# A decoder trunk on one core: the hand-over from the up product to the down product of the ConvFFN is reordered

## The chip, the cores and the metric

The kernel runs on one NeuronCore of a Trainium2 chip. Its engines are PE (TensorE, matrix products), DVE (VectorE), ACT (ScalarE), POOL (GpSimd) and SP (SyncE, which here only issues DMAs). Each engine works through its own instructions in a fixed order and waits, instruction by instruction, on semaphores; ACT and POOL can issue DMAs too. The metric is the device time of one execution in microseconds (us).

## The reference

One inference step of a decoder trunk in float32: 1,024 prompt tokens behind 16 meta tokens, and 8 × 4 sample tokens, through a convolution layer, a shared latent-attention layer, and a ConvFFN in each of the two layers. What matters here is the ConvFFN, which both layers run:

```python
def conv_ffn(x, prefix, w_up, w_dw, w_down):
    h, tail = causal_dwconv(x @ w_up, prefix, w_dw)      # x: tokens x 1024, w_up: 1024 x 5632, 3 taps
    g, u = jnp.split(h, 2, axis=-1)                      # 2816 each
    return (jax.nn.silu(g) * u) @ w_down, tail           # w_down: 2816 x 1024

for layer in range(2):
    ...
    d_p, t_p = conv_ffn(rms_norm(hp, norm_ffn[layer]), zero_ffn, *f_params)
    d_s, t_s = conv_ffn(rms_norm(hs, norm_ffn[layer]), state_ffn_conv[layer], *f_params)
    hp, hs = hp + d_p, hs + d_s
```

The rows `tail` (the last up-projected rows) are outputs as well, `o["tail_f"]` in the kernel.

## The kernel before

Every float32 product is made of three: an operand is split into a rounded high part and the remainder (`split`: ACT writes the high part at L134, DVE the low part at L135), and PE adds high·high, high·low and low·high. So every operand of a product costs one ACT and one DVE instruction before PE can use it. Tokens lie along the free axis, 1,074 of them in layer 0 (1,062 in layer 1), features along the 128 partitions.

**The up product (`rise`).** 22 blocks f of 128 gate features and 128 up features. Each block is a product of 2 × 2 quarters done with seven products (L735) in place of eight; the operands are `b11`, `b21`, `b22`, `t1` to `t4` (made once, in the pool `xc`), and `product` runs them in the order t1, t2, b21, t3, then the next block's b11, then t4, b22. `keep` copies a partial sum out of PSUM on ACT (L743: `u2`, `u3`, `p1`), `join` adds it on DVE into the two rows `ub` of the block (L746). A product that goes on in the same PSUM bank waits for that copy: t3 for the copy of `u2`.

`tail(f)` then does, for the two rows: a store of the tail to `o["tail_f"]` (L700, SP's queue), the first tap on ACT (`c`, L703), two more taps on DVE (L705), the sample tokens on POOL, silu on ACT (L717), the product of the two on DVE (L718), and the store of the result to DRAM (`d_a[f]`, L719, SP's queue). The tiles `c` come from a pool of two buffers, which the RMS of the attention's cache (`nk`, eight odd blocks f of layer 0) borrows too, and gives back when its store `d_ss<-nk` has landed.

**The down product (`fall`).** It begins when `rise` is over, and its tiles are taken in the pools that `open_x` opens anew. `act(f)` loads `d_a[f]` back (L851, `raw`, three buffers) and splits it into `xh`/`xl`; `weight` loads a block of w_down (L151) and splits it into `wh`/`wl`. The 22 blocks f are the contraction now, in three groups (`BLOCKS`): 8, 7 and 7. In a group, for each of the eight output tiles, `gemm` (L170) runs over the blocks k of the group, three chunks of the tokens for each of the three products, so nine matmuls per k; DVE adds the result to `x` (L866), which is loaded back from `d_r` (L860).

```python
        for f in range(BLOCKS[0][1]):
            act(f)
        ...
            for ot in range(KD):
                w = self.weight(a["wdn"][layer, ot][:, f0 * 128:(f0 + n) * 128], n * 128)
                _, ps = self.gemm(w, [acts[f][0] for f in range(f0, f0 + n)], ...)
```

"The switch" below is the stretch between the last b22 product of `rise` and PE at full pace in `fall`. The order of each engine's instructions is set by a scheduler when the program is built, from the order of the code, priorities (`high_priority`) and ordering edges (`follow`, which cost no semaphore); where a tile lies, and so which earlier work it must wait for, follows from the order in which pools are opened and tiles taken.

Of the kernel before, what the change touches and what calls it, by code (L numbers as in the profile page):

```python
# [9 lines left out]
F32 = mybir.dt.float32  # L10
# [107 lines left out]
class Prog:  # L118
# [40 lines left out]

    def gemms(self, ws, mh, ml, off, tn, every=0):  # L160
        nc = self.nc
        ch = tn // 3
        cnt = 0
        ps = [self.pp.tile([128, 3, 512], F32, name="ps") for _ in ws]
        n = len(mh)
        for k in range(n):
            for w, p in zip(ws, ps):
                for i, (s, m) in enumerate(((w[0], mh), (w[0], ml), (w[1], mh))):
                    for c in range(3):
                        nc.tensor.matmul(p[:, c, :ch], s[:, k * 128:(k + 1) * 128], m[k][:, off + c * ch:off + (c + 1) * ch],  # L170
                                         start=k == 0 and i == 0, stop=k == n - 1 and i == 2)
                        cnt += 1
                        if every and cnt % every == 0:
                            next(self.fill, None)
        return [(p, p[:, :, :ch]) for p in ps]
# [114 lines left out]

    def open_x(self, tw=T0):
        self.tw = tw
        self.es_r, self.es_x, self.es_w, self.es_p = [self.top.enter_context(ExitStack()) for _ in range(4)]
        self.rp = self.pool(self.es_r, "rp", 1)
        self.xa, self.xb = [self.pool(self.es_x, n, 1) for n in ("xa", "xb")]
        self.xp = self.pool(self.es_w, "xp", 1)
        self.wp = self.pool(self.es_w, "wp", 2)
        self.tp = self.pool(self.es_w, "tp", 3)
        self.sp = self.pool(self.es_w, "sp", 1)

# [10 lines left out]
    def xhl(self, k):  # L311
        return self.xp.tile([128, self.tw], F32R, name=f"xh{k}"), self.xp.tile([128, self.tw], F32R, name=f"xl{k}")

# [198 lines left out]
    def layer_norm(self, ys):  # L512
# [15 lines left out]
        with self.tc.high_priority(PRIO):  # L528
            for k in range(KD):
                nc.vector.scalar_tensor_tensor(out=v3(ys[k]), in0=mu[:, :, :ch], scalar=-1.0 / D, in1=v3(ys[k]), op0=ALU.mult, op1=ALU.add)  # L530
            for k in range(KD):
                if k == 0:
                    self.sq_add(sq, ys[k], 0, T0)
                    continue
                q = self.xp.tile([128, self.tw], F32R, name=f"xl{k}").bitcast(F32)
                nc.scalar.activation(q, ys[k], AF.Square)
# [74 lines left out]
    def ffn(self, layer, xs, rstd, tn, done, extra=None):  # L611
        with ExitStack() as es:
            self.rise(es, layer, xs, rstd, tn, extra)
        self.es_r.close()
        self.open_x(self.tw)
        self.open_pp(self.es_p)
        with ExitStack() as es:
            self.fall(es, layer, tn, done)

    def rise(self, es, layer, xs, rstd, tn, extra):  # L620
# [20 lines left out]
        def operand(name, k, src, tag=None):  # L641
            h, l = [xc.tile([128, 536], F32R, name=f"{name}{x}{k}", tag=f"{tag or name}{x}{k}")[:, :hw] for x in "hl"]
            B[name, k] = h, l
            return self.split(h, l, src)[1]
# [49 lines left out]
        def tail(f):  # L694
# [3 lines left out]
            for j, ub in enumerate(ubs):  # L698
                t = f + j * NF
                nc.sync.dma_start(o["tail_f"][layer, t], ub[:, pe - 2:])  # L700
                nc.gpsimd.tensor_copy(sb[:, j, 16:48], ub[:, pe:])  # L701
                c = self.tp.tile([128, T0], F32, name="c", tag="c")[:, :tn]
                nc.scalar.activation(c, ub, AF.Copy, scale=wd[:, t, 2:3])  # L703
                for tap in (1, 0):
# [13 lines left out]
            nc.vector.tensor_tensor(out=cs[1], in0=cs[0], in1=cs[1], op=ALU.mult)  # L718
            nc.sync.dma_start(self.d_a[f][:, :tn], cs[1])  # L719
            if extra is not None and f % 2 and f < 16:  # L720
# [92 lines left out]
        self.es_w.close()  # L813
        xc = self.pool(es, "xc", 1, "right")
        pb = self.pool(es, "pb", 8, space=PSUM)
# [27 lines left out]
    def fall(self, es, layer, tn, done):  # L843
# [5 lines left out]
        def act(f):  # L849
            raw = self.tp.tile([128, 1152], F32, name="raw", tag="c")[:, :tn]  # L850
            nc.sync.dma_start(raw, self.d_a[f][:, :tn])  # L851
            h, l = self.xhl(f) if f < BLOCKS[0][1] else [ar.tile([128, T0], F32R, name=n) for n in ("ah", "al")]
            self.split(h[:, :tn], l[:, :tn], raw)
            acts[f] = h, l

        for f in range(BLOCKS[0][1]):
            act(f)
        xs = [self.x32(k, tn) for k in range(KD)]
        for k in range(KD):
            nc.sync.dma_start(xs[k], self.d_r[k][:, :tn])  # L860
        for i, (f0, n) in enumerate(BLOCKS):
            nxt = list(range(BLOCKS[i + 1][0], sum(BLOCKS[i + 1]))) if i + 1 < len(BLOCKS) else []
            for ot in range(KD):
                w = self.weight(a["wdn"][layer, ot][:, f0 * 128:(f0 + n) * 128], n * 128)
                _, ps = self.gemm(w, [acts[f][0] for f in range(f0, f0 + n)], [acts[f][1] for f in range(f0, f0 + n)], 0, tn)
                nc.vector.tensor_tensor(out=v3(xs[ot]), in0=ps, in1=v3(xs[ot]), op=ALU.add)  # L866
                if not nxt and i == len(BLOCKS) - 1:
                    done(ot, xs[ot])
                if nxt:
                    act(nxt.pop(0))  # L870
# [920 lines left out]
```

## Time and profile before

| | us |
|---|---|
| median of 3 runs | 2890.12 (2887.99 to 2891.42) |
| the profiled execution's own time | 2889.14 |
| its span in the trace | 2887.4 |
| PE busy | 2696.6 (93% of the span) |
| DVE, ACT, POOL busy | 1912.6, 1385.1, 624.6 |
| layer 0: rise, then the switch | up to 1080.25, then to about 1094 |
| layer 1: rise, then the switch | up to 2611.66, then to about 2626 |

Times of the trace count from the start of the span. An engine's timeline gives start, duration and instruction, with the engine's idle time before it and what ended it in brackets; "x3" is three instructions of one kind in a row, the duration that of all three. Consecutive matmuls overlap in the records, so their pace is read from start to start. "PEclk" of a window is the granted clock of TensorE as a share of full speed (its two levels are 1.2 and 2.4 GHz).

### The profile page before, as it was taken

To read this page: it belongs to the slowest core of one execution; us is meant where nothing else is said; L and a number is where in the kernel's file an instruction comes from. 1 tells how busy PE (TensorE), PEld (TensorE's weight loads), DVE (VectorE), ACT (ScalarE), POOL (GpSimd) and SP (SyncE) were. 2 spreads that over 40 slices of the span, in tenths; PEclk is the share of its full clock that TensorE was granted. 3 is DMA by queue.
4 is the path that set the end of the run, shared out by engine and by line. 5 is a ranking of instruction groups with operands and counts; after the bars stand their busy time and mean duration, and the time that the engine had idled before them with its cause. 6 is when DMAs were issued, how large, how long until landed. Compare 5 with 4: busy or idle time off the path is not lost.

```text
span 2887.4 us, 47547 instructions
## 1 busy us (share of the span) xinstructions
PE 2696.6 (93%) x16916; PEld 2475.4 (86%) x16916; DVE 1912.6 (66%) x3516; ACT 1385.1 (48%) x4074; POOL 624.6 (22%) x875
## 2 busy tenths in 40 slices
PE   7999986999999999999789999988999999998999
PEld 5888864999999999999666776656999999998999
DVE  7899997468888865135577767655458777775231
ACT  6777778335454543023555564645325544453010
POOL 1457542013232320001101211100004323230000
PEclk9999997989999999999889999978999999999999
DMA  4111110412222226122100001347502222217122
GB/s 132 54 39 56 41 45 19 150 47 81 92 84 91 83 87 237 42 91 88 36 5 23 30 16 31 118 123 223 185 31 71 76 85 77 85 63 263 46 83 73
DMA packets 127779, 238.32 MB, mean 83 GB/s; under 512 B 39778, under 2 KB 81140, under 8 KB 127412
## 3 DMA queue, kind: packets, MB, share of 16 engines
q1 hardware_dynamic: 122836, 226.42, 24.4%
q0 software_dynamic: 3264, 8.30, 0.9%
q8 instruction: 133, 2.18, 0.3%
q14 instruction: 106, 0.87, 0.1%
q10 hardware_dynamic: 1440, 0.55, 0.1%
HBM read 183.90 MB, written 51.31 MB: 81 GB/s over the span
## 4 chain that ended last, share of the span: by engine, by line
PE 80%; DVE 8%; ACT 5%; issue 2%; DMA 2%; SPq 1%; POOL 0%; ACTq 0%; DVEq 0%; POOLq 0%
PE ps L735 29%; PE ps L170 23%; PE pk L596 4%; PE v L1244 4%; PE g L388 3%; PE ps L784 3%; PE p L146 2%; ACT qq L608 2%; PE ps L192 2%; DVE a L481 2%; PE ps L938 2%; PE p L1254 1%; PE p L1256 1%; PE p L1257 1%; PE s L1214 1%
## 5 line engine op out<-in xcount | busy, mean ns | idle before, releaser
L134 ACT ACTIVATE wh<-raw 128x512 fp32r<-128x512 f32 (+2 forms) x256 | 191.6, 751 | 579.4 <-PE ps L170 372.3
L135 DVE TENSOR_TENSOR wl<-raw,wh 128x512 fp32r<-128x512 f32 (+2 forms) x244 | 201.2, 828 | 108.1 <-ACT wh L134 108.0
L866 DVE TENSOR_TENSOR x<-ps,x 128x1074 f32<-128x1074 f32 (+1 forms) x48 | 61.0, 1270 | 297.7 <-PE ps L170 297.7
L705 DVE SCALAR_TENSOR_TENSOR c<-ub,c,c 128x1040 f32<-128x1040 f32 (+1 forms) x176 | 225.0, 1312 | 27.0 <-ACT c L703 27.0
L608 ACT ACTIVATE qq<-pk 128x64 f32<-128x64 f32 x936 | 198.1, 247 | 78.9 <-PE pk L596 78.3
L608 ACT ACTIVATION_READ_ACCUMULATOR qq<-pk 128x1 f32 x936 | 194.2, 232 | 0.1
L701 POOL COPY sb<-ub 128x32 f32<-128x32 f32 x88 | 78.3, 891 | 530.5 <-DVE ub L746 480.2
L1244 PE MATMUL v<-pf,vf 128*128 128x512 f32 (+4 forms) x448 | 175.9, 476 | 11.6 <-ACT pf L1261 11.3
L603 POOL TENSOR_TENSOR sq<-sq 128x256 f32<-128x256 f32 x198 | 130.4, 660 | 185.4 <-ACT sq L599 178.1
L170 PE MATMUL ps<-xh,wh 128*128 128x358 f32 (+1 forms) x672 | 149.7, 332 | 18.5 <-ACT wh L134 17.4
L596 PE MATMUL pk<-ukh,ch 128*128 128x512 f32 x256 | 115.8, 453 | 48.5 <-ACT qq L608 17.2
L1261 ACT ACTIVATE pf<-p 128x512 f32<-128x512 f32 (+4 forms) x224 | 99.2, 450 | 123.2 <-DVE p L1259 99.0
L170 PE MATMUL ps<-xl,wh 128*128 128x358 f32 (+1 forms) x672 | 148.4, 329 | 0.0
L170 PE MATMUL ps<-xh,wl 128*128 128x358 f32 (+1 forms) x672 | 147.5, 328 | 0.6 <-DVE wl L135 0.4
L170 PE MATMUL ps<-al,wh 128*128 128x358 f32 (+1 forms) x672 | 146.9, 327 | 0.0
L170 PE MATMUL ps<-ah,wh 128*128 128x358 f32 (+1 forms) x672 | 146.4, 326 | 0.0
L170 PE MATMUL ps<-ah,wl 128*128 128x358 f32 (+1 forms) x672 | 146.2, 325 | 0.0
L481 DVE SCALAR_TENSOR_TENSOR a<-u,c,a 128x512 f32<-128x512 f32 x200 | 137.9, 744 | 0.0
L170 PEld LDWEIGHTS ps<-xh,wh 128*128 128x128 f32 x672 | 118.0, 193 | 20.6 <-ACT wh L134 17.8
L388 PE MATMUL g<-xh,wh 128*128 128x358 f32 x336 | 111.8, 333 | 17.9 <-DVE u L372 16.2
L703 ACT ACTIVATE c<-ub,c 128x1074 f32<-128x1074 f32 (+1 forms) x88 | 101.1, 1184 | 55.7 <-DVE ub L746 45.6
L170 PEld LDWEIGHTS ps<-xl,wh 128*128 128x128 f32 x672 | 118.2, 192 | 0.9
(583 smaller groups left out, 9080.1 us busy)
## 6 DMA issues: line engine op xcount, KB each, us to landing
raw<-wup SPq DMA_DIRECT2D x88, 512.0 KB, 3.6
pg<-ctn SPq DMA_DIRECT2D x128, 192.0 KB, 2.7
raw<-wdn SPq DMA_DIRECT2D x32, 448.0 KB, 3.5
raw<-pw SPq DMA_DIRECT2D x24, 512.0 KB, 3.8
d_a<-c SPq DMA_DIRECT2D x22, 537.0 KB, 3.3
raw<-d_a SPq DMA_DIRECT2D x22, 537.0 KB, 5.2
d_a<-c SPq DMA_DIRECT2D x22, 531.0 KB, 2.8
raw<-d_a SPq DMA_DIRECT2D x22, 531.0 KB, 5.0
```

The lines of the kernel that those rows point to most:

```text
L134: return (nc.scalar.activation(h, src, AF.Copy), (eng or nc.vector).tensor_tensor(out=l, in0=src, in1=h.bitcast(F32), op=ALU.subtract))
L135: (eng or nc.vector).tensor_tensor(out=l, in0=src, in1=h.bitcast(F32), op=ALU.subtract))
L170: nc.tensor.matmul(p[:, c, :ch], s[:, k * 128:(k + 1) * 128], m[k][:, off + c * ch:off + (c + 1) * ch], start=k == 0 and i == 0, stop=k == ...
L388: nc.tensor.matmul(p[:, 0], x[:, k * 128:(k + 1) * 128], m[k][:, t * ch:t * ch + ch], start=k == 0 and i == 0, stop=k == KD - 1 and i == 2)
L481: nc.vector.scalar_tensor_tensor(out=p[:, :ND] if j == n - 1 else acc, in0=x[:, j:j + ND], scalar=w[:, j:j + 1], in1=p[:, :ND] if j == 1 e ...
L596: nc.tensor.matmul(ps, s[:, j, :], m[:, 512 * c:512 * c + 512], start=i == 0, stop=i == 2)
L603: nc.gpsimd.tensor_tensor(out=v[:, :, :n], in0=v[:, :, :n], in1=v[:, :, n:2 * n], op=ALU.add)
L608: nc.scalar.activation(q, ps[:, 64 * h:64 * h + 64], AF.Square, accum_out=ss[:, p, 8 * c + h:8 * c + h + 1])
L703: nc.scalar.activation(c, ub, AF.Copy, scale=wd[:, t, 2:3])
L705: nc.vector.scalar_tensor_tensor(out=c[:, 2:pe], in0=ub[:, tap:tap + pe - 2], scalar=wd[:, t, tap:tap + 1], in1=c[:, 2:pe], op0=ALU.mult, ...
L735: nc.tensor.matmul(ps, w[:, s], m[:, lo:hi], start=first and k == 0 and i == 0, stop=k == KD // 2 - 1 and i == 2, skip_group_check=True)
L1244: nc.tensor.matmul(o[:, at_:], vf[:m, b, c], p[:m, :512 - at_], start=b == 0, stop=last)
```

## The change

1. `gemms` takes `last`. The first two output tiles of the first group are computed together: for each k both outputs, and only the last two k one output after the other.
2. `fall` issues the first two weights and the eight activations of the first group under high priority, with the tiles `xh`/`xl` (`room`) taken ahead; the loads of `x` follow the last load of an activation.
3. The pools are ordered by when their memory comes free: for `fall`, `wp` (weights) and `tp` are opened first, `xp` is split into `xp0`, `xp1`, `xp2`, and the operands of `rise` lie in three pools (t4, b22), (b21, t3), (b11, t1, t2) in place of `xc`.
4. The 88 tail stores go to ACT's DMA queue, right behind the first tap; the 44 stores of `d_a` go to POOL's.

```diff
-    def gemms(self, ws, mh, ml, off, tn, every=0):
+    def gemms(self, ws, mh, ml, off, tn, every=0, last=0):
...
-        for k in range(n):
-            for w, p in zip(ws, ps):
+        both = list(zip(ws, ps))
+        for k, (w, p) in [(k, x) for k in range(n - last) for x in both] + [(k, x) for x in both for k in range(n - last, n)]:
...
-    def open_x(self, tw=T0):
+    def open_x(self, tw=T0, order=("xp0", "xp1", "xp2", "wp", "tp", "sp")):
...
-        self.xp = self.pool(self.es_w, "xp", 1)
-        self.wp = self.pool(self.es_w, "wp", 2)
-        self.tp = self.pool(self.es_w, "tp", 3)
-        self.sp = self.pool(self.es_w, "sp", 1)
+        for n in order:
+            setattr(self, n, self.pool(self.es_w, n, {"wp": 2, "tp": 3}.get(n, 1)))
...
+    def xpool(self, k):
+        return self.xp0 if k < 2 else self.xp1 if k < 5 else self.xp2
...
-        self.open_x(self.tw)
+        self.open_x(self.tw, ("wp", "tp", "sp", "xp0", "xp1", "xp2"))
...
-                nc.sync.dma_start(o["tail_f"][layer, t], ub[:, pe - 2:])
...
-                nc.scalar.activation(c, ub, AF.Copy, scale=wd[:, t, 2:3])
+                x = nc.scalar.activation(c, ub, AF.Copy, scale=wd[:, t, 2:3])
+                self.follow(nc.scalar.dma_start(o["tail_f"][layer, t], ub[:, pe - 2:]), [x])
...
-            nc.sync.dma_start(self.d_a[f][:, :tn], cs[1])
+            nc.gpsimd.dma_start(self.d_a[f][:, :tn], cs[1])
...
-        xc = self.pool(es, "xc", 1, "right")
+        xc = {}
+        for names in (("t4", "b22"), ("b21", "t3"), ("b11", "t1", "t2")):
+            p = self.pool(es, names[0], 1, "right")
+            xc.update({n: p for n in names})
...
-        for f in range(BLOCKS[0][1]):
-            act(f)
+        room = {f: self.xhl(f) for f in range(BLOCKS[0][1])}
+        with self.tc.high_priority(PRIO):
+            ws = [weight(0, ot) for ot in range(2)]
+            for f in range(BLOCKS[0][1]):
+                act(f)
...
-            nc.sync.dma_start(xs[k], self.d_r[k][:, :tn])
+            self.follow(nc.sync.dma_start(xs[k], self.d_r[k][:, :tn]), [acts["dma"]])
...
+            ps = self.gemms(ws, mh, ml, 0, tn, last=2) if i == 0 else []
```

How the built program moves, at three places. SP's queue at the switch of layer 0, before (`raw<-wdn` is a weight of the down product, `raw<-d_a` an activation, `ub`, `c` and `x` the tiles named above):

```order
L860 DMA x1_15292<-d_r_66 128x1074
L719 DMA d_a_67<-c_14936 128x1074
L700 DMA o_tail_f<-ub_14811 128x34
L851 DMA raw_15243<-d_a_67 128x1074
L851 DMA raw_15249<-d_a_67 128x1074
L700 DMA o_tail_f<-ub_14810 128x34
L851 DMA raw_15255<-d_a_67 128x1074
L151 DMA raw_15307<-wdn 128x1024
L151 DMA raw_15393<-wdn 128x1024
L851 DMA raw_15261<-d_a_67 128x1074
```

and with the change (its own line numbers run up to 12 higher):

```order
L663 DMA raw_14829<-wup 128x1024
L663 DMA raw_14965<-wup 128x1024
L751 DMA sb_14822<-stf 128x2x16
L151 DMA raw_15281<-wdn 128x1024
L151 DMA raw_15287<-wdn 128x1024
L855 DMA raw_15293<-d_a_67 128x1074
L855 DMA raw_15297<-d_a_67 128x1074
L855 DMA raw_15301<-d_a_67 128x1074
L151 DMA raw_15501<-wdn 128x1024
L151 DMA raw_15587<-wdn 128x1024
```

The first two weights stand right behind the last loads of `rise`, ahead of the activations; the stores between them have left SP's queue. The same place in layer 1, with the semaphores that each row waits for:

```order
L855 DMA raw_33043<-d_a_67 128x1062 [waits DMAHW7_49,DMASW2_49,PE_49]
L855 DMA raw_33047<-d_a_67 128x1062 [waits DMAHW0_49,DMASW3_49,PE_49]
L855 DMA raw_33051<-d_a_67 128x1062 [waits DMAHW1_49,DMASW4_49]
L855 DMA raw_33055<-d_a_67 128x1062 [waits DMAHW2_49,DMAHW7_49,DMASW5_49,DVE_49]
L855 DMA raw_33059<-d_a_67 128x1062 [waits DMAHW0_49,DMAHW3_49,DMASW6_49,DVE_49]
L855 DMA raw_33063<-d_a_67 128x1062 [waits DMAHW1_49,DMAHW4_49,DMASW7_49,DVE_49]
L855 DMA raw_33067<-d_a_67 128x1062 [waits DMAHW2_49,DMAHW5_49,DMASW0_49,DVE_49]
L151 DMA raw_33031<-wdn 128x1024 [waits DVE_49]
L151 DMA raw_33037<-wdn 128x1024
L855 DMA raw_33071<-d_a_67 128x1062 [waits DMAHW3_49,DMASW1_49,DVE_49]
```

Here the two weights stand behind seven activations, and the first of them waits for DVE: its buffer covers memory that the last `join` of `rise` (`ub<-ps,u2`) reads. DVE's order at the switch of layer 0, before (the rows L746 and L705 are the last joins and taps of `rise`):

```order
L746 TENSOR_TENSOR ub<-ps,u_15068 128x268 x2
L746 TENSOR_TENSOR ub<-ps,u_14991 128x268 x2
L705 SCALAR_TENSOR_TENSOR c<-ub,c_58,c 128x1040 x3
L135 TENSOR_TENSOR xl_15246<-raw,xh_15245 128x1074
L705 SCALAR_TENSOR_TENSOR c<-ub,c_58,c 128x1040
L135 TENSOR_TENSOR xl_15252<-raw,xh_15251 128x1074
L135 TENSOR_TENSOR xl_15258<-raw,xh_15257 128x1074
L718 TENSOR_TENSOR c<-c 128x1074
L135 TENSOR_TENSOR wl<-raw,wh 128x1024 x2
L135 TENSOR_TENSOR xl_15264<-raw,xh_15263 128x1074
```

and with the change:

```order
L135 TENSOR_TENSOR wl<-raw,wh 128x1024 x2
L747 TENSOR_TENSOR ub<-ps,u_15082 128x268 x2
L135 TENSOR_TENSOR xl_15266<-raw,xh_15265 128x1074
L135 TENSOR_TENSOR xl_15268<-raw,xh_15267 128x1074
L747 TENSOR_TENSOR ub<-ps,u_15005 128x268
L135 TENSOR_TENSOR xl_15270<-raw,xh_15269 128x1074
L747 TENSOR_TENSOR ub<-ps,u_15005 128x268
L706 SCALAR_TENSOR_TENSOR c<-ub,c_58,c 128x1040 x4
L135 TENSOR_TENSOR xl_15272<-raw,xh_15271 128x1074
L135 TENSOR_TENSOR xl_15274<-raw,xh_15273 128x1074
L719 TENSOR_TENSOR c<-c 128x1074
```

The low parts of the two weights have moved from behind the last taps and the multiply to ahead of the last four joins, and three of the activations' low parts to ahead of the taps.

## Rows read from the trace of the kernel before

**Rows 1.** Windows: rise and switch of layer 0, switch of layer 1.
```profile
core 0: us, PE busy (x) PEld busy (x) DVE busy (x) ACT busy (x) POOL busy (x), PEclk, DMA share, GB/s
640.00:1080.00 440.00, 440.00 (x3570) 440.00 (x3568) 361.34 (x559) 219.31 (x387) 138.48 (x211) 1.00 0.27 85
1080.00:1094.00 14.00, 5.18 (x21) 4.50 (x20) 12.39 (x11) 9.33 (x9) 4.82 (x7) 0.63 0.81 253
2611.00:2626.00 15.00, 6.25 (x25) 5.58 (x24) 12.99 (x12) 9.89 (x10) 4.77 (x7) 0.66 0.79 254
```

**Rows 2.** Waits of PE, whole span: total us, times, longest.
```profile
PE ps L170 <- ACT wh L134: 17.4, 2, 8.7
```

**Rows 3.** Timeline of PE at layer 0's switch: start, us, instruction, idle before.
```profile
1079.97 0.28 PE L735 MATMUL ps<-b22h,wl 128*128 128x268 f32 x1
1088.99 1.26 PE L170 MATMUL ps<-xh,wh 128*128 128x358 f32 x3 [8.74 <-ACT wh L134]
...
1093.02 0.77 PE L170 MATMUL ps<-xh,wl 128*128 128x358 f32 x3
1093.63 0.65 PE L170 MATMUL ps<-xh,wh 128*128 128x358 f32 x3
1094.12 0.66 PE L170 MATMUL ps<-xl,wh 128*128 128x358 f32 x3
```

**Rows 4.** Timeline of ACT at the same place.
```profile
1068.75 1.10 ACT L717 ACTIVATE c<-c 128x1074 f32<-128x1074 f32 x1
...
1080.82 2.27 ACT L703 ACTIVATE c<-ub,c 128x1074 f32<-128x1074 f32 x2 [1.61 <-DVE ub L746]
...
1087.90 1.99 ACT L134 ACTIVATE wh<-raw 128x1024 fp32r<-128x1024 f32 x2
```

**Rows 5.** Timeline of DVE at the same place.
```profile
1082.05 3.77 DVE L705 SCALAR_TENSOR_TENSOR c<-ub,c,c 128x1040 f32<-128x1040 f32 x3 [1.32 <-ACT c L703]
1085.74 1.32 DVE L135 TENSOR_TENSOR xl<-raw,xh 128x1074 fp32r<-128x1074 f32 x1
...
1091.76 2.35 DVE L135 TENSOR_TENSOR wl<-raw,wh 128x1024 fp32r<-128x1024 f32 x2
```

**Rows 6.** Timeline of SP's DMA issues at the same place.
```profile
1081.67 0.85 SPq L151 DMA_DIRECT2D raw<-wdn  x2
1087.09 3.91 SPq L851 DMA_DIRECT2D raw<-d_a  x3
```

**Rows 7.** Timeline of PE at layer 1's switch.
```profile
2611.38 0.28 PE L735 MATMUL ps<-b22h,wl 128*128 128x264 f32 x1
2620.34 1.25 PE L170 MATMUL ps<-xh,wh 128*128 128x354 f32 x3 [8.67 <-ACT wh L134]
...
2625.99 0.64 PE L170 MATMUL ps<-xl,wh 128*128 128x354 f32 x3
```

**Rows 8.** Timeline of ACT at layer 1's switch.
```profile
2612.23 2.25 ACT L703 ACTIVATE c<-ub,c 128x1062 f32<-128x1062 f32 x2 [1.62 <-DVE ub L746]
```

**Rows 9.** Timeline of DVE at layer 1's switch.
```profile
2611.71 0.43 DVE L746 TENSOR_TENSOR ub<-ps,u 128x264 f32<-128x264 f32 x1 [2.53 <-PE ps L735]
```

**Rows 10.** DMA issues of the page: KB each, median us to landing.
```profile
raw<-wdn SPq DMA_DIRECT2D x16, 512.0 KB, 5.0
...
d_o<-o POOLq DMA_DIRECT2D x7, 512.0 KB, 3.3
```

**Rows 11.** Tile d_o: its DMA issues from ACT's queue, ns min/median/max.
```profile
L1317 ACTq DMA_DIRECT2D d_o<-o x8: 326/398/451, 1573.7 to 1893.8; - x8
```

**Rows 12.** Timeline of ACT in the rise, an odd f of layer 0.
```profile
862.67 0.37 ACT L743 ACTIVATE u<-ps 128x268 f32<-128x268 f32 x1
```

**Rows 13.** Timeline of PE there.
```profile
864.02 0.28 PE L735 MATMUL ps<-t3h,wh 128*128 128x268 f32 x1
```

**Rows 14.** Timeline of SP at the latents, before the attention.
```profile
1411.94 0.39 SPq L997 DMA_DIRECT2D o_c_p<-cts  x1
```

**Rows 15.** Timeline of PE there.
```profile
1408.81 0.34 PE L146 MATMUL p<-wq0h,qll 128*128 128x384 f32 x1
```

More of the change, by code (lines that the diff above doesn't have):

```diff
@@ L165, in gemms @@
         n = len(mh)
-        for k in range(n):
-            for w, p in zip(ws, ps):
[L168 to L174, printed above, removed]
+        both = list(zip(ws, ps))
+        for k, (w, p) in [(k, x) for k in range(n - last) for x in both] + [(k, x) for x in both for k in range(n - last, n)]:
+            for i, (s, m) in enumerate(((w[0], mh), (w[0], ml), (w[1], mh))):
+                for c in range(3):
+                    nc.tensor.matmul(p[:, c, :ch], s[:, k * 128:(k + 1) * 128], m[k][:, off + c * ch:off + (c + 1) * ch],
+                                     start=k == 0 and i == 0, stop=k == n - 1 and i == 2)
+                    cnt += 1
+                    if every and cnt % every == 0:
+                        next(self.fill, None)
         return [(p, p[:, :, :ch]) for p in ps]
@@ L311, in xhl @@
     def xhl(self, k):
-        return self.xp.tile([128, self.tw], F32R, name=f"xh{k}"), self.xp.tile([128, self.tw], F32R, name=f"xl{k}")
+        return [self.xpool(k).tile([128, self.tw], F32R, name=f"x{x}{k}") for x in "hl"]
+    def xpool(self, k):
+        return self.xp0 if k < 2 else self.xp1 if k < 5 else self.xp2
     def conv_phase(self):
@@ L534, in layer_norm @@
                     continue
-                q = self.xp.tile([128, self.tw], F32R, name=f"xl{k}").bitcast(F32)
+                q = self.xpool(k).tile([128, self.tw], F32R, name=f"xl{k}").bitcast(F32)
                 nc.scalar.activation(q, ys[k], AF.Square)
@@ L641, in operand @@
         def operand(name, k, src, tag=None):
-            h, l = [xc.tile([128, 536], F32R, name=f"{name}{x}{k}", tag=f"{tag or name}{x}{k}")[:, :hw] for x in "hl"]
+            h, l = [xc[tag or name].tile([128, 536], F32R, name=f"{name}{x}{k}", tag=f"{tag or name}{x}{k}")[:, :hw] for x in "hl"]
             B[name, k] = h, l
@@ L850, in act, with weight @@
             raw = self.tp.tile([128, 1152], F32, name="raw", tag="c")[:, :tn]
-            nc.sync.dma_start(raw, self.d_a[f][:, :tn])
-            h, l = self.xhl(f) if f < BLOCKS[0][1] else [ar.tile([128, T0], F32R, name=n) for n in ("ah", "al")]
+            acts["dma"] = nc.sync.dma_start(raw, self.d_a[f][:, :tn])
+            h, l = room[f] if f < BLOCKS[0][1] else [ar.tile([128, T0], F32R, name=n) for n in ("ah", "al")]
             self.split(h[:, :tn], l[:, :tn], raw)
             acts[f] = h, l
-        for f in range(BLOCKS[0][1]):
-            act(f)
+        def weight(i, ot):
+            f0, n = BLOCKS[i]
+            return self.weight(a["wdn"][layer, ot][:, f0 * 128:(f0 + n) * 128], n * 128)
+        room = {f: self.xhl(f) for f in range(BLOCKS[0][1])}
[3 more added lines that the diff above has]
+                act(f)
         xs = [self.x32(k, tn) for k in range(KD)]
         for k in range(KD):
-            nc.sync.dma_start(xs[k], self.d_r[k][:, :tn])
+            self.follow(nc.sync.dma_start(xs[k], self.d_r[k][:, :tn]), [acts["dma"]])
         for i, (f0, n) in enumerate(BLOCKS):
             nxt = list(range(BLOCKS[i + 1][0], sum(BLOCKS[i + 1]))) if i + 1 < len(BLOCKS) else []
+            mh, ml = [[acts[f][j] for f in range(f0, f0 + n)] for j in range(2)]
+            ps = self.gemms(ws, mh, ml, 0, tn, last=2) if i == 0 else []
             for ot in range(KD):
-                w = self.weight(a["wdn"][layer, ot][:, f0 * 128:(f0 + n) * 128], n * 128)
-                _, ps = self.gemm(w, [acts[f][0] for f in range(f0, f0 + n)], [acts[f][1] for f in range(f0, f0 + n)], 0, tn)
-                nc.vector.tensor_tensor(out=v3(xs[ot]), in0=ps, in1=v3(xs[ot]), op=ALU.add)
+                x = ps[ot][1] if ot < len(ps) else self.gemm(weight(i, ot), mh, ml, 0, tn)[1]
+                nc.vector.tensor_tensor(out=v3(xs[ot]), in0=x, in1=v3(xs[ot]), op=ALU.add)
                 if not nxt and i == len(BLOCKS) - 1:
```

## The prediction

> **What bounds the kernel.** I looked first at the busy shares: PE works 93% of the span, so a gain needs a place where PE is not at full pace. I then asked for PE's waits over the span. In the rises there is nothing: PE is busy in all of 440 us, at a granted clock of 1.00 (the 2.4 GHz level), with DVE and ACT below it [rows 1]. The two longest waits of one kind are those at the two switches: 17.4 us in two waits, the longest 8.7, the first L170 matmul waiting for ACT's `wh` [rows 2]. So the third view is the timeline of the switches, engine by engine.
>
> Layer 0: the last matmul of the rise ends at 1079.97 + 0.28 = 1080.25; the first of the down product starts at 1088.99, 8.74 us later. PE then runs slower: it reaches its steady pace, three matmuls in 1094.12 − 1093.63 = 0.49 us (0.163 each), at 1093.63, and has done five triples by then, the fifth held up for `wl` until 1093.02 [rows 3]. The clock of 1080 to 1094 is 0.63: PE idled, and the clock fell towards its lower level [rows 1].
>
> Why is `wh` late? SP issues the loads of the weights only at 1081.67 [rows 6], a load lands in 5.0 us [rows 10], and ACT has the first taps and three `xh` ahead of it and reaches `wh` at 1087.90 [rows 4]. DVE, with four taps, three `xl` and the multiply ahead, reaches `wl` at 1091.76 [rows 5].
>
> **What the change does at layer 0's switch.** The weights' loads go right behind the last loads of the rise, many us ahead. ACT can split both after the last but one silu, which ends at 1068.75 + 1.10 = 1069.85 [rows 4]; DVE makes the two `wl` (2.35 us together [rows 5]) ahead of the last four joins. So k = 0 is complete before 1080.25, and PE goes on without a gap.
>
> Then each further activation must keep ahead of PE. The pair of outputs doubles the work per k: 18 matmuls × 0.163 = 2.94 us, so PE reads `xl` of block k at 1080.25 + 2.94 k + 0.49. Blocks 0 to 2 are split ahead of the last taps. Block 3 is the tight one. Its `xl` stands behind all four taps; they start at 1082.05 and take 1.26 each (3.77 for three [rows 5]), so they end at 1087.1, with the second of ACT's first taps 0.4 later than now (one store issue between, 326 to 451 ns [rows 11]) and not in the way; with 1.3 for `xl` [rows 5] it is there at 1088.4. PE wants it at 1080.25 + 8.82 + 0.49 = 1089.6: 1.2 us to spare. Block 4 comes at 1089.7 (wanted 1092.5), block 5 behind the multiply at 1092.2 (wanted 1095.4), the rest at 1.3 a piece against 2.94.
>
> The same 15 matmuls that are done at 1093.63 now are then done at 1080.25 + 15 × 0.163 = 1082.70: **10.9 us gained**.
>
> **Layer 1's switch.** There SP's order puts the weights behind seven activations, and the first weight's load waits for DVE's last join of the rise, which ends at 2611.71 + 0.43 = 2612.14 [rows 9]. It can't be ahead of the switch; the change doesn't do there what it says. Issued at 2612.2 and 5.0 on its way [rows 10], it lands at 2617.2. ACT meanwhile does a first tap (2.25 for two, from 2612.23 [rows 8]), a store issue of 0.4 [rows 11], `xh` 5 (1.0, as a `wh`), the second tap, another issue, `xh` 6, and comes to `wh` at 2617.4: it is ACT's queue that sets it, by 0.2 us. A `wh` takes 1.0 (1.99 for two [rows 4]); PE restarts at 2618.5 where it now does at 2620.34 [rows 7], at the lower clock again (0.66 in this switch [rows 1]). DVE's `wl` of output 1 stands behind `xl` 4, four taps in all, `xl` 5 and 6 and the first `wl`: from 2612.14, at 1.2 to 1.3 each and two short waits for ACT, it ends at 2623.3, as I count it; the last triple of k = 0 then takes at most twice 0.49 at the lower clock, to 2624.3. The trace has 18 matmuls done at 2625.99 [rows 7]: **1.7 us gained** (0.5 to 2.5: the landing a few us off either way, or the waits for ACT longer).
>
> **What else it moves, and what hides it.**
> - SP loses 132 DMA issues. SP holds nobody up in the rises, where PE has no idle time at all: nothing.
> - ACT gets 88 store issues of 0.33 to 0.45 us [rows 11], two per f, behind the first taps. Where this can reach PE is the odd f of layer 0 that carry `nk`: there ACT's second first tap waits for a store and comes late, and the copy of `u2` stands behind it, at 862.67 for 0.37 [rows 12]; t3 overwrites that bank at 864.02 [rows 13]. The slack is 864.02 − 863.04 = 1.0 us, the two issues take 0.65 to 0.9. It holds, narrowly: nothing, at worst a few tenths in each of eight f.
> - POOL gets 44 stores of 537 KB. The nearest row, POOL's own 512 KB stores in the attention, lands in 3.3 us [rows 10]; nobody in the rise waits for `d_a` within that: nothing.
> - The pool split costs no instruction. But the order in which the scheduler places other phases shifts. At the latents SP's loads of the query weights now stand behind the last store of `cts`, issued at 1411.94 [rows 14]; twelve query matmuls, which now run before that in PE's waits at 0.34 each [rows 15], follow later. Up to 12 × 0.34 = 4.1 us could be lost; PE has other waits there which they can still fill: I put down nothing and keep 4 for the range.
>
> **Sum.** 10.9 + 1.7 = 12.6. The profiled execution's own time is 2889.14, which gives 2876.5; the median of the runs lies 0.98 above that execution: **2877.5 us**, with its own range 2874 (layer 1's upper end and a better landing elsewhere) to 2881 (4 us lost at the latents).
>
> **Rivals.**
> - *Both switches close.* If layer 1's weights did come in time, its 18 matmuls would end at 2611.66 + 18 × 0.163 = 2614.6, 11.4 earlier than 2625.99: 22.3 in all, 2867.8. The build's wait for the last join speaks against it. Chance 0.06.
> - *The gain is given back.* Block 3's 1.2 us go (a load of `d_a` late, the taps slower), PE stops once more in layer 0, and the clock falls with it; a stop of 2 us and 2 to 4 us at up to half pace cost 3 to 4. Or the latents lose their 4.1 and the eight odd f 0.3 each. 2880 to 2886. For it: the slack is small, and the order of many other instructions moved. Chance 0.22.
> - *It doesn't do it in layer 0 either*: the weights there wait for a buffer that I misjudged, and each switch gains the 1.7. 2889.14 − 3.4 + 0.98 = 2886.7. Against it: in the changed SP order they stand ahead of all that belongs to the down product. Chance 0.07.
> - *Slower: ACT's queue holds up the rise.* The place is the copy of `u2` in the eight odd f. If a store issue on ACT takes not 0.4 but t, PE stops 2t − 1.0 per f: from t = 0.5 something is lost, at t = 1.3 (8 × 1.6 = 12.8) the whole gain is gone, and at t = 2 it ends at 2877.5 + 8 × 3.0 = 2901.5. That issues of 1.3 us exist shows SP, three in 3.91 [rows 6]; that ACT's took 0.33 to 0.45 speaks against it. Chance 0.05.
> - *Slower: POOL's stores starve.* If a store waits on POOL until DVE gives way, the `c` that it holds comes free late, ACT's first tap with it, and `u2` behind that. DVE is busy 361 of 440 us in the rise [rows 1]. At worst, with no slack at all, each of the 44 loses the whole delay: 0.3 us apiece eat the gain, 1 us makes 2877.5 + 44 = 2921.5. The row of POOL's stores, 3.3 to land beside a busy DVE [rows 10], speaks against it. Chance 0.03. The Trainium skill's page "SBUF — State Buffer", section "Who interferes with whom", has the rule behind this one: a DMA from GpSimd's queue can be kept from writing its descriptors while DVE holds the port that they share, in its two-port modes, and the page advises the queues of ACT or SP instead, against this part of the change. The same section says that tensor_tensor has no such mode, and the DVE work of the rise is nearly all of that kind; by that half of the rule the stores would land as now. No row of before shows a `d_a` store on POOL.
>
> **The numbers.** The forecast has 0.57; its range and both neighbours lie in 2867 to 2886, which leaves out the last three rivals (0.15) and a sliver of the second. About 0.2% (5.8 us) is what a measurement of this kernel can tell from no change, so faster means below 2884.3: 0.57 + 0.06 + 0.16 of the second rival = 0.79. Within: the rest of the second and the third, 0.13. Slower: 0.08.
>
> **What would show it.** Right: PE goes from L736 to L170 without idle time near 1080, clock 1.00 on both sides; in layer 1 a wait for `wh` of about 7 us, two short ones for `wl`, and SP's weight loads just after the last join. PE idle in the odd f's, ahead of t3, would show the ACT rival; first taps that wait for `d_a` the POOL rival; a wait for `xl` some 9 us into layer 0's down product the second. The prediction is wrong if layer 0 keeps a gap of over 2 us, if layer 1's gap is below 5, or if over 4 us go anywhere outside the switches.

## The result, and the profile after

| | before | with the change |
|---|---|---|
| median | 2890.07 us (4 runs) | 2870.11 us (2866.27 to 2873.55, 4 runs) |
| ratio to before, 95% interval | | 0.9931 (0.9914 to 0.9948) |
| span of the profiled execution | 2887.4 | 2868.6 |

20.0 us less, where 12.6 were forecast (2877.5, range 2867 to 2886). All times compared here and below are of fast runs; one run of the kernel before, 4331.74 us at a granted clock of 0.554, is left out. Where did the time go? PE's waits for the down product in the change, over the span (total us, times, longest), against one row before [rows 2]:

```profile
PE ps L170 <- ACT wh L134: 7.3, 1, 7.3
...
PE ps L170 <- DVE x L878: 0.8, 1, 0.8
```

One of the two long waits is gone, the other is shorter, and a small one is new. Windows of the two switches in the change:

```profile
core 0: us, PE busy (x) PEld busy (x) DVE busy (x) ACT busy (x) POOL busy (x), PEclk, DMA share, GB/s
1080.00:1094.00 14.00, 14.00 (x87) 14.00 (x87) 11.01 (x9) 7.41 (x7) 5.34 (x8) 1.00 0.59 182
2596.00:2611.00 15.00, 7.80 (x37) 7.55 (x38) 14.46 (x13) 9.83 (x10) 8.03 (x8) 0.77 0.97 356
```

In layer 0 PE is busy throughout and the granted clock stays at the 2.4 GHz level, where it was 0.63 [rows 1]. Layer 1 still has a stop, with a clock of 0.77. The hand-over of layer 0 in PE's timeline:

```profile
1079.06 0.29 PE L736 MATMUL ps<-b22h,wl 128*128 128x268 f32 x1
1079.18 0.65 PE L170 MATMUL ps<-xh,wh 128*128 128x358 f32 x3
1079.67 0.65 PE L170 MATMUL ps<-xl,wh 128*128 128x358 f32 x3
...
1088.06 1.15 PE L170 MATMUL ps<-xh,wh 128*128 128x358 f32 x6
1089.04 0.65 PE L170 MATMUL ps<-xl,wh 128*128 128x358 f32 x3
...
1103.78 0.73 PE L170 MATMUL ps<-xh,wh 128*128 128x358 f32 x3 [0.77 <-DVE x L878]
```

The down product starts 0.12 us behind the start of the last b22 matmul, and three of its matmuls start every 0.49 us from the first [rows 3 show the gap of 8.74 in their place]. What DVE does meanwhile:

```profile
1070.96 2.35 DVE L135 TENSOR_TENSOR wl<-raw,wh 128x1024 fp32r<-128x1024 f32 x2
...
1081.18 4.98 DVE L706 SCALAR_TENSOR_TENSOR c<-ub,c,c 128x1040 f32<-128x1040 f32 x4 [1.32 <-ACT c L703]
1086.09 2.45 DVE L135 TENSOR_TENSOR xl<-raw,xh 128x1074 fp32r<-128x1074 f32 x2
...
1101.16 1.28 DVE L135 TENSOR_TENSOR al<-raw,ah 128x1074 fp32r<-128x1074 f32 x1 [4.58 <-ACT ah L134]
1102.36 1.27 DVE L878 TENSOR_TENSOR x<-ps,x 128x1074 f32<-128x1074 f32 x1
```

Both `wl` are made by 1073.3, some 7 us before PE needs the first. The `xl` of block 3, the first of the two from 1086.09, is ready at about 1087.3. Block 3's turn comes after 18 triples of 0.49 us, at 1088.06; it begins with two triples on `xh`, one for each output, and PE reads the `xl` at 1089.04: 1.7 us to spare, 1.2 were forecast. The last two rows are the new small wait: the first output's add stands behind the low part of an activation of the second group, and the third output waits for the PSUM that this add frees.

Layer 1, in PE's timeline and in DVE's, SP's and ACT's:

```profile
2595.59 0.28 PE L736 MATMUL ps<-b22h,wl 128*128 128x264 f32 x1
2603.20 1.25 PE L170 MATMUL ps<-xh,wh 128*128 128x354 f32 x3 [7.33 <-ACT wh L134]
...
2607.03 0.65 PE L170 MATMUL ps<-xh,wl 128*128 128x354 f32 x3
2607.51 0.65 PE L170 MATMUL ps<-xh,wh 128*128 128x354 f32 x3
2608.00 0.65 PE L170 MATMUL ps<-xl,wh 128*128 128x354 f32 x3
```
```profile
2595.91 0.43 DVE L747 TENSOR_TENSOR ub<-ps,u 128x264 f32<-128x264 f32 x1 [1.00 <-PE ps L736]
```
```profile
2596.37 0.81 SPq L151 DMA_DIRECT2D raw<-wdn  x2
```
```profile
2602.10 1.06 ACT L134 ACTIVATE wh<-raw 128x1024 fp32r<-128x1024 f32 x1 [1.34 <-DMA raw<-wdn]
```

The weights' loads leave SP 0.03 us after the last join ends (2595.91 + 0.43 = 2596.34), 5.7 us later ACT splits the first, and PE starts 7.33 us after the last b22 in place of 8.67 [rows 7].

To place the gain I cut each profiled execution at the same matmuls, read from PE's timeline: the last b22 of each rise (the rise itself is counted from its first L735 matmul, L736 in the change), the last L170 matmul of each down product, the last 64-column matmul of the attention's samples (L1562, L1574 in the change) and the last matmul of the output projection (L146). "Down 0" and "down 1" run from the last b22 to the last L170 matmul of the layer, "attention" from there to the samples' last, "projection" from there to its own last. The kernels of the experiments are in the same table.

| kernel | last b22 of layer 0 at | down 0 | attention | projection | down 1 |
|---|---|---|---|---|---|
| before | 1080.25 | 271.94 | 675.34 | 34.88 | 269.79 |
| the change, first profile | 1079.34 | 262.01 | 673.71 | 31.46 | 267.57 |
| change_again, change_third | 1080.28, 1080.72 | 261.97, 262.32 | 674.44, 676.56 | 32.96, 31.55 | 268.88, 267.65 |
| queues_only | 1080.64 | 271.94 | 674.58 | 35.48 | 270.08 |
| xp_only | 1075.24 | 271.94 | 675.02 | 33.66 | 269.21 |
| no_pools | 1074.84 | 271.14 | 675.35 | 31.65 | 268.49 |
| no_queues | 1075.47 | 262.66 | 675.83 | 31.70 | 267.69 |
| no_pair | 1074.71 | 260.93 | 674.73 | 32.51 | 268.36 |
| forced_order | 1083.26 | 268.21 | 674.31 | 31.96 | 267.57 |
| fix_layer1, again | 1083.88, 1077.21 | 262.19, 262.08 | 673.08, 674.21 | 31.79, 31.48 | 259.37, 260.70 |
| fix_both, again | 1081.92, 1080.73 | 260.91, 261.04 | 668.58, 671.27 | 31.52, 32.00 | 259.69, 258.22 |

In the first profile: 9.9 us at layer 0's switch, 2.2 at layer 1's, 3.4 in the projection, 1.6 in the attention, and the rest of the 18.8 ahead of layer 0's switch (0.9) and at the end.

### The profile page after: what moved, and what is told of

It is laid out like the page before. It is cut to its first block, busy times and chain, and to the rows that moved or that the text cites. A ratio compares the mean times of both kernels' runs of the same rounds, so it can differ in the third digit from the quotient of the medians.

```text
span 2868.6 us, 47477 instructions
## 1 busy us (share of the span) xinstructions
PE 2684.6 (94%) x16916; PEld 2465.2 (86%) x16916; DVE 1915.9 (67%) x3516; ACT 1388.0 (48%) x4074; POOL 650.3 (23%) x919
## 4 chain that ended last, share of the span: by engine, by line
PE 80%; DVE 9%; ACT 5%; SPq 3%; issue 2%; DMA 2%; POOL 0%; ACTq 0%; DVEq 0%; POOLq 0%
PE ps L736 29%; PE ps L170 22%; PE v L1256 4%; PE pk L597 4%; PE g L389 3%; PE ps L785 3%; PE p L146 2%; DVE a L482 2%; PE ps L192 2%; ACT qq L609 2%; PE ps L950 1%; SPq L556 1%; SPq L554 1%; PE p L1266 1%; PE p L1268 1%
## 5 line engine op out<-in xcount | busy, mean ns | idle before, releaser
L170 PE MATMUL ps<-xh,wh 128*128 128x358 f32 (+1 forms) x672 | 149.1, 330 | 9.2 <-ACT wh L134 7.3
L170 PE MATMUL ps<-xl,wh 128*128 128x358 f32 (+1 forms) x672 | 147.6, 328 | 0.0
L170 PE MATMUL ps<-xh,wl 128*128 128x358 f32 (+1 forms) x672 | 147.2, 327 | 0.4 <-DVE wl L135 0.4
L170 PE MATMUL ps<-al,wh 128*128 128x358 f32 (+1 forms) x672 | 146.9, 327 | 0.0
L170 PE MATMUL ps<-ah,wh 128*128 128x358 f32 (+1 forms) x672 | 146.4, 326 | 0.0
L170 PE MATMUL ps<-ah,wl 128*128 128x358 f32 (+1 forms) x672 | 146.2, 325 | 0.0
L170 PEld LDWEIGHTS ps<-xh,wh 128*128 128x128 f32 x672 | 116.9, 191 | 11.5 <-ACT wh L134 7.8
L134 ACT ACTIVATE wh<-s 128x512 fp32r<-128x512 f32 x120 | 75.8, 632 | 96.9 <-PE ps L736 96.4
```

What stands on the lines that cost most here:

```text
L134: return (nc.scalar.activation(h, src, AF.Copy), (eng or nc.vector).tensor_tensor(out=l, in0=src, in1=h.bitcast(F32), op=ALU.subtract))
```

## The experiments

**What the moved stores do.** queues_only is the kernel before with these lines and nothing else:

```diff
-                nc.sync.dma_start(o["tail_f"][layer, t], ub[:, pe - 2:])
-                nc.scalar.activation(c, ub, AF.Copy, scale=wd[:, t, 2:3])
+                x = nc.scalar.activation(c, ub, AF.Copy, scale=wd[:, t, 2:3])
+                self.follow(nc.scalar.dma_start(o["tail_f"][layer, t], ub[:, pe - 2:]), [x])
...
-            nc.sync.dma_start(self.d_a[f][:, :tn], cs[1])
+            nc.gpsimd.dma_start(self.d_a[f][:, :tn], cs[1])
```

> The kernel before, with the tail stores on ACT's queue and the stores of d_a on POOL's, and nothing else. Theory: nothing hides behind the moved stores, both rises stay as they are (layer 0's without PE idle time), the switches too; total as before, within 2 us. Rival ACT: PE waits ahead of t3 in the odd f of layer 0, 0.1 to 0.5 us each. Rival POOL: ACT's first taps wait for stores of d_a, and the rise of layer 0 grows by several us.

Measured: 2886.08 us, ratio to before 0.9983 (0.9969 to 0.9998); PE has no wait in the rise, both switches keep 8.7 us, down 0 is 271.94 as before. Its stores, by the views of the tiles `d_a` and `o_tail_f` over the rise of layer 0 (issue time in ns, min/median/max; then us to landing):

```profile
L719 POOL DMA_DIRECT2D d_a<-c x22: 573/597/723, 672.7 to 1092.5; - x22
...
DMA to landing us min/median/max: 3.2/3.5/9.3
```
```profile
L703 ACTq DMA_DIRECT2D o_tail_f<-ub x42: 338/339/1184, 660.5 to 1064.0; - x42
...
DMA to landing us min/median/max: 1.4/1.6/4.6
```

(The landings of the first also hold eight loads of `d_a`.) An issue on ACT takes 0.34 us, a store from POOL lands in 3.5 beside a DVE that is busy 82% of the rise. Both slower rivals fall. By the Trainium skill's page "SBUF — State Buffer", section "Who interferes with whom", a DMA from GpSimd's queue can starve beside DVE's two-port modes but not beside tensor_tensor; the second half agrees with this trace, and the first no run here shows. Of DVE's 367 us in the rise, summed over its instructions, 235 are tensor_tensor and 127 scalar_tensor_tensor, the taps above all, on which the section says nothing; the stores landed in time beside both.

no_queues is the reverse: the change, with those stores on SP's queue again.

> The change, with tail stores and d_a stores on SP's queue again. Theory: the moved stores are worth nothing; layer 0's switch stays without a gap, total 2868 to 2872. Rival (SP's queue, where a store that waits for the last join stands ahead of the loads of activations, holds these up): xl of the blocks from 6 on comes late, PE waits in the pair, 2 to 5 us lost, total 2873 to 2875.

Measured: 2874.83 us, 0.9957 (0.9944 to 0.997). No gap at layer 0's switch, down 0 0.65 longer (the third output waits 1.4 for the add in place of 0.8), down 1 the same (267.69). The theory holds for the stretches that it speaks of. The median lies above its range and in the rival's (2873 to 2875), but the waits for `xl` in the pair that the rival rests on aren't in the trace; and the profiled execution, 2870.52, is in the theory's range, with an attention of 675.83, where the change's own goes up to 676.56. Whether the queues are worth a few us elsewhere the totals don't tell.

**What the pools do.** no_pools is the change with these lines put back:

```diff
-        xc = {}
-        for names in (("t4", "b22"), ("b21", "t3"), ("b11", "t1", "t2")):
-            p = self.pool(es, names[0], 1, "right")
-            xc.update({n: p for n in names})
+        p = self.pool(es, "xc", 1, "right")
+        xc = {n: p for n in ("t4", "b22", "b21", "t3", "b11", "t1", "t2")}
...
-        self.open_x(self.tw, ("wp", "tp", "sp", "xp0", "xp1", "xp2"))
+        self.open_x(self.tw)
```

> The change, with the operands of rise in one pool again and the pools of fall in the old order (xp stays split). Theory (memory decides): the first weight's load waits for the last b22 matmul in both layers, so PE stops at layer 0's switch again for 6 to 8 us and the clock falls; some 9 us of layer 0's gain are gone, total 2877 to 2881. Rival (order decides, priority and place in the queues): the switch stays closed, total 2870.

Measured: 2881.43 us, 0.998 (0.9969 to 0.9991), 0.4 above the theory's range and far from the rival's 2870. In PE's timeline layer 0 stops again, and SP's timeline shows why (the last b22 ends at 1074.84):

```profile
1083.13 2.16 PE L170 MATMUL ps<-xh,wh 128*128 128x358 f32 x6 [8.29 <-ACT xh L134]
```
```profile
1074.87 0.81 SPq L151 DMA_DIRECT2D raw<-wdn  x2
```

The loads still stand ahead of those of the activations, under the same priority, but they leave 0.03 us after the last b22 matmul, which reads the memory under them. In the change they left 32 us ahead of its end (1079.35):

```profile
1047.01 1.07 SPq L151 DMA_DIRECT2D raw<-wdn  x2
```

Down 0 is 271.14: 9.1 of the 9.9 us are gone. It is memory, not order, that closes the switch; which of the two pool edits, these lines don't tell.

**What the order of the pair does.** In no_pair the first two outputs are written one after the other:

```diff
-            ps = self.gemms(ws, mh, ml, 0, tn, last=2) if i == 0 else []
+            ps = [self.gemm(x, mh, ml, 0, tn) for x in ws] if i == 0 else []
```

> The change, with the first two outputs of the first group one after the other. Theory (the pair halves PE's demand for activations): PE starts without a gap at layer 0's switch, but wants xl of block 3 at about 5 us behind the last b22, 3 us before DVE has it, and that of block 7 6 to 7 us too early; PE waits 6 to 8 us in small pieces in layer 0, perhaps with a fall of the clock on top; layer 1, where wl of the first output is what is late, loses under 2. Layer 0's stretch from the last b22 to the end of the down product 268 to 271 in place of 262. Rival (DVE gets ahead all the same): 262 to 264.

Measured: 2869.20 us, 0.9931 (0.9913 to 0.9949), down 0 260.93, no wait in it. Theory and edit both missed: the scheduler interleaves the two outputs by itself once both weights are there (its order has blocks 0 to 2 of the first, 0 and 1 of the second, then both in turns). It ends the first output earlier than the written order, so the wait for PSUM is gone too, 1.1 us. To hold the outputs apart, PE's order has to be fixed by hand, which forced_order does:

```diff
+                with self.manual():
+                    ps = [self.gemm(x, mh, ml, 0, tn) for x in ws]
```

> The change, with PE's order fixed by hand in the first group: all blocks k of the first output, then all of the second (in no_pair the scheduler had interleaved the two outputs by itself). Theory (interleaving halves PE's demand for activations and is what keeps layer 0's switch closed): PE starts without a gap, then waits for xl of block 3 (about 3 us) and again, for 0.5 to 2 us each, for blocks 5 to 7, 6 to 7 us in all; layer 0's stretch from the last b22 to the end of the down product is 267 to 270 in place of 262. Rival (DVE is ahead anyway): 261 to 263. Layer 1, where PE waits for the weights, within 1.5 of the change for both.

Measured: 2881.46 us, 0.9956 (0.9934 to 0.9977); down 0 268.21, 6.2 longer. PE's waits from 1060 to 1120:

```profile
PE ps L170 <- DVE xl L135: 4.2, 3, 3.1
PE ps L170 <- ACT xh L134: 0.2, 1, 0.2
```

The first wait is the 3.1 us that was worked out for block 3; 4.4 are waits, 6 to 7 were expected, and most of the rest goes with the clock: 0.94 in the 26.7 us behind the last b22 (1083.3 to 1110) against 1.00 in those of the change, 1.6 us at full pace. The total, 2881.46, holds more than that: its stretch ahead of layer 0's switch is 3.9 longer than in the change's first profile. So interleaving is needed, but writing it out was not.

**Why layer 1 stays open.** fix_layer1 leaves 2,800 bytes per partition free ahead of the weights' pool in layer 1. Its edit does a second thing that it was not meant to do: the name `PAD` was taken, by a spacer of 13,888 bytes per partition among the pools of the attention's samples, and that one shrinks to 700 bytes.

```diff
+PAD = 700
...
-PAD = 13888
+PAD = 700
...
+            if n == "pad":
+                self.pad.tile([128, PAD], F32, name="pad")
...
-        self.open_x(self.tw, ("wp", "tp", "sp", "xp0", "xp1", "xp2"))
+        self.open_x(self.tw, (("pad",) if layer else ()) + ("wp", "tp", "sp", "xp0", "xp1", "xp2"))
```

> The change, with 2800 bytes left free ahead of the weights' pool in layer 1, so that the first weight's buffer no longer covers memory that the last join reads. Theory: layer 1's switch closes as layer 0's did; 18 matmuls are done 2.9 us after the last b22 in place of 12.1, so 9.2 us less, total about 2861. Rival (the loads are early but DVE or ACT is late, since the tail's work is the same): the wait shrinks by 3 to 5 us only, total 2865 to 2867.

Measured: 2866.04 us, 0.9923 (0.9904 to 0.9942). SP's timeline ahead of layer 1's switch, PE's at it, and the window behind it:

```profile
2567.81 1.07 SPq L152 DMA_DIRECT2D raw<-wdn  x2
```
```profile
2600.03 0.29 PE L739 MATMUL ps<-b22h,wl 128*128 128x264 f32 x1
2600.15 0.67 PE L171 MATMUL ps<-xh,wh 128*128 128x354 f32 x3
2600.65 0.65 PE L171 MATMUL ps<-xl,wh 128*128 128x354 f32 x3
```
```profile
2600.00:2615.00 15.00, 15.00 (x95) 15.00 (x94) 11.72 (x11) 7.58 (x8) 5.37 (x8) 1.00 0.60 184
```

The weights' loads leave 32 us before the last b22 ends, where they left 0.5 us behind it in the change, and the stop is gone; down 1 is 259.37, 8.2 less than in the change (9.2 expected; a wait of 0.9 us for the add is now in this layer too). The total is 5 us above what was expected; in the profiled execution 4.5 us of that lie ahead of layer 0's switch, where PE's and SP's orders are those of the change.

The smaller spacer shows in SP's loads of the samples' pages (`pg`): behind the first 32 of the 128 SP stops for 30 to 32 us in the four executions of fix_layer1 and fix_both, and for 36 to 39 in the ten of the other kernels. From their first matmul on `pg` to the last of the samples those four take 122.9 to 124.4 us, the three of the change 124.8 to 125.3. So the totals and the attention of fix_layer1 and fix_both hold this effect too, and no run has it apart. Layer 1's switch does not rest on it, as far as the traces show: behind the page loads SP's order is the change's again up to layer 1's own switch, where the weights' loads have moved.

**The last 0.8 us.** fix_both adds one ordering edge to fix_layer1, from DVE's add of the first output to the low part behind which it stood:

```diff
-            self.split(h[:, :tn], l[:, :tn], raw)
+            self.follow(self.split(h[:, :tn], l[:, :tn], raw)[1], after)
...
-                    act(nxt.pop(0))
+                    act(nxt.pop(0), [y] if i == 0 and ot == 0 else ())
```

> The change with the 2800 free bytes of fix_layer1, and the first low part of the second group ordered behind DVE's add of the first output, which frees the PSUM that the third output waits for. Theory: the wait of 0.8 us for that add goes in both layers, 0.7 less in each stretch (261.4 and 258.6), total 1 to 2 us below fix_layer1. Rival (the low part was needed as early as it was): the second group waits for it instead, no gain.

Measured: 2857.92 us, 0.988 (0.9862 to 0.9899). Down 0 is 1.3 less than in fix_layer1, down 1 0.3 more; but the attention took 668.58, 4.5 less, with the same order on PE, SP and POOL there. Both have the small spacer, so that it isn't. Three kernels on one chip show what of that comes again:

> The change as it is, beside the two next on one chip: 0.993 to 0.995 of the time before, layer 1's stretch 267.5 to 269.

> fix_layer1 on the same chip: layer 1's stretch 259.4 again, total 8 us below the change, if the difference of that stretch carries through to the end.

> fix_both on the same chip: its stretches 260.9 and 259.5. Its order on PE, POOL and SP is that of fix_layer1 outside the down product, so if the 4.5 us that it was faster in the attention were an accident of that execution, its attention takes 673 to 675 now and its total is 1 to 2 us below fix_layer1; if they belong to the kernel, 668 to 669 again and 5 to 7 us below.

Measured: 2873.61 us, 0.9933 (0.9917 to 0.9949); 2861.32, 0.9896 (0.9878 to 0.9914); 2861.61, 0.9893 (0.9874 to 0.9912). In the medians fix_layer1 is 12.3 us faster than the change. In the profiled executions closing layer 1 is 7.0 of that (8.2 in the first pair), 3.5 lie ahead of layer 0's switch, where PE's and SP's orders are the same, and 2.3 in the attention, where the smaller spacer works too; so closing layer 1 is worth 7 to 8 us, and not the 12.3. The edge is worth nothing that the totals show: 1.0 in down 0, 2.5 in down 1 this time. Its attention, 671.27, lies between the two guesses, 1.8 below the lowest of the kernels without it; whether anything of that is its own stays open. Either version beats both kernels of this study.

**The output projection.** xp_only is the kernel before, with `xp` alone split:

```diff
-        self.xp = self.pool(self.es_w, "xp", 1)
+        self.xp0, self.xp1, self.xp2 = [self.pool(self.es_w, n, 1) for n in ("xp0", "xp1", "xp2")]
```

> The kernel before, with xp alone split into xp0, xp1, xp2. Theory A (the output projection's 3.4 us come from PE's order there, which the split changes: the small po products stand behind the first large ones and so run after the clock has risen): the projection, from its first matmul of 354 columns to its last, is 3 to 4 us shorter than in the kernel before, both switches keep their 8.7 us waits, total about 2886.7. Theory B (they come from what else the change moved, the arrival of the sample work): projection unchanged, total 2890.

Measured: 2884.24 us, 0.999 (0.9977 to 1.0003): the total can't tell. The timelines of PE can. The small `po` products, 24 in all, in the kernel before (first and last rows), then in xp_only from the second on (one runs earlier):

```profile
2033.59 0.26 PE L146 MATMUL po<-oth,s 128*128 128x64 f32 x1
...
2038.35 0.40 PE L146 MATMUL po<-oth,s 128*128 128x64 f32 x1
2038.56 0.64 PE L146 MATMUL ps<-xh,wh 128*128 128x354 f32 x1
```
```profile
2033.00 0.19 PE L146 MATMUL po<-otl,s 128*128 128x64 f32 x1
...
2035.38 0.28 PE L146 MATMUL po<-oth,s 128*128 128x64 f32 x1
```

5.0 us before, about 2.5 now: the scheduler puts them behind twenty of the large products, and by then the clock has risen. That by itself saves nothing, for the large products that run ahead of them in their place run at half pace instead; what saves is that the slow stretch is shorter. Its matmuls start every 0.295 us in place of 0.163 from 2031.8 to about 2042 before (10 us), from 2029.3 to 2042.4 in queues_only, which has the old order too (13), and from 2026.3 to 2032.8 in xp_only (6.4); in all twelve executions with the split it is 3 to 7. With the small products in it PE works on at the slow pace for longer; that this is what their place does fits all fourteen executions, but only the split moved them, and no run moves them alone. From its first large matmul to its last the projection takes 29.6 us (32.7 before), as theory A had it; in this execution 1.9 us of it went into a longer first wait for `wh` (4.10 in place of 2.23). Every kernel with the split takes 31.5 to 33.7 for the projection, the two without it 34.9 and 35.5.

**The spread.**

> The change as it is, a second time, beside the others of this call. Both theories: the same stages as in the first profile within 0.3 us (rise 414.5, layer 0 from the last b22 to the end of the down product 262.0, layer 1 267.6); what differs between executions is the stretch ahead of layer 0's rise. If that stretch differs by several us while these stages agree, the spread of the totals is from there.

Measured: 2874.89 us, 0.9946 (0.9933 to 0.9959). The rise takes 414.54 us in all three executions of the change and down 0 262.0 to 262.3, as expected; down 1, 267.6 to 268.9, ranges over 1.3 where 0.3 was expected, the attention over 2.9, the projection over 1.5, and the stretch ahead of layer 0's switch over 1.4 only, where several us were looked for (9.2 over all kernels of the table, though no theory has them differ there). The spread of totals comes from all four. In xp_only and no_pools 2.7 of the 9.2 are in the rise: the same number of matmuls, 3,360, without idle time, takes 411.81. In xp_only they stand in the order of the kernel before, and nothing in the edit touches them; these runs don't tell why.

## Why the prediction was right, point by point

- *The range.* 2870.11 lies in 2867 to 2886, but not in the forecast's own 2874 to 2881; the range reaches down to 2867 for the rival in which both switches close, and that didn't come. What was foreseen is the two switches, 12.1 us in the first profile for 12.6. That the other 8 us of the 20.0, which no term has, still ended inside the range is luck. One of the prediction's own signs of being wrong was over 4 us anywhere outside the switches: no single stretch has more than 3.4 of the first profile's 18.8, but together it is 6.7.
- *Layer 0's switch, 10.9.* Measured 9.9 (271.94 to 262.01). The mechanism was as forecast, down to block 3's margin (1.7 us for 1.2). The step "the rest at 1.3 a piece against 2.94" looked only at what goes into the pair. What comes out was left out: both outputs end late, and the third waits 0.8 for the add that frees its PSUM.
- *Layer 1's switch, 1.7.* Measured 2.2 (and 0.9 to 2.1 in the other two executions). PE restarted 7.33 us after the last b22 for 6.8 forecast, since the landing took 5.7 and so set it, not ACT's queue, which waited 1.3 us for it; but the two short waits for `wl` didn't come, the clock was back at full pace by 2607.03, and the 18th matmul was done 12.1 us after the last b22 for 12.6. The two misses nearly cancel.
- *The stores, nothing.* Right; queues_only shows rise and switches unmoved. The reading that nearly all of DVE's work in the rise is tensor_tensor was wrong, it is two thirds; the rival fell all the same.
- *The pool split "costs no instruction … I put down nothing".* This is the term that was mis-sized: with the split of `xp` the small products of the output projection stand elsewhere and the slow stretch there is shorter, 3.2 us on the means (35.2 to 32.0). The prediction looked for moved work only at the latents; the output projection isn't in it.
- *The latents, up to 4.1 lost.* Nothing of it came: from the end of layer 0's down product to the first score matmul (`s<-c,k`) it is 88.0 us in the three executions of the change and 89.1 before. The attention takes 673.7 to 676.6 in the change and 674.6 to 675.3 in the kernels of the old order.
- *Both switches close* was a rival with 0.06; the build's wait spoke against it and decided. fix_layer1 shows what it would have given: 10.4 less than before in that stretch (269.79 to 259.37; 9.1 in its second execution) where the prediction has 11.4.
- *Open.* Down 0, down 1 and the projection give 9.8 + 1.9 + 3.2 = 14.9 us, on the means of the executions (queues_only counted with the kernel before); the medians differ by 20.0, 16.8 and 17.5 in the three comparisons. The 2 to 5 us between lie in stretches that vary by as much from one execution to the next, and no run here places them.

## What to carry to other kernels

A hand-over between two products is closed by memory first: a load can start only when the last reader of its buffer is done, so take the buffers of the next stage's first weights from what the previous stage frees first, and look in the built program at what each early load waits for, in every layer: here the same code closed one layer's switch and left the other's open. Ask then how fast the engine behind the wait will want its operands, and let two outputs share them until the split is ahead. After a wait, let large products go first: with small ones among them the slow stretch lasted 10 to 13 us here, without them 3 to 7.

## What the runs showed of the hardware that was not expected

- A stretch in which PE never waits repeats closely between executions and chips (the rise takes 414.53 or 414.54 in twelve of the fourteen executions), while the attention ranges from 668.6 to 676.6 and the stretch ahead of layer 0's switch from 1074.7 to 1083.9. But it isn't free of surprises: xp_only and no_pools have 411.81, and all of the 2.7 is in the 1,120 high·high matmuls, each followed 2.4 ns sooner. A difference of 0.1% is read from stretches, not from totals.
- The same wait of 2.2 us ahead of the projection left PE's pace in two ways. In the kernel before, PE's timeline shows the first six large matmuls near full pace, and the fall 2.1 us behind that wait, 0.8 behind a second one of 0.67:

```profile
2031.45 0.33 PE L146 MATMUL ps<-xl,wh 128*128 128x354 f32 x1
2031.62 0.40 PE L146 MATMUL ps<-xh,wl 128*128 128x354 f32 x1
2031.82 0.50 PE L146 MATMUL ps<-xh,wh 128*128 128x354 f32 x1
...
2042.46 0.33 PE L146 MATMUL ps<-xl,wh 128*128 128x354 f32 x1
```

In the change the second matmul has the slow 0.50 already, and the fast 0.32 is back 5.7 us later:

```profile
2017.69 0.50 PE L146 MATMUL ps<-xl,wh 128*128 128x354 f32 x1
...
2023.34 0.32 PE L146 MATMUL ps<-xh,wh 128*128 128x354 f32 x1
```

So before, the slow pace held from 2031.8 to about 2042, the whole of the small products in it (granted clock 0.50 in 2031.8 to 2042). It isn't the order that made it come late: in queues_only, with the same order and a wait of 2.15, the second matmul has 0.50 already, and the slow pace holds to 2042.4, 11.8 us of it in unbroken work from 2030.59. Why, these runs don't tell.
